# An MLP block on one core: x of three pairs transposed by DMA in place of TensorE, and two groups of sums moved forward

## The chip, the cores and the metric

The kernel runs on one core of one Trainium2 chip. The metric is the device time of one execution in microseconds (us), lower is better; each figure is a median over several executions.

## The reference

x is (8, 1024, 1024), taken as 8192 rows of 1024; w1 is 1024 x 4096, w2 is 4096 x 1024, all float32.

```python
h = x @ w1
h = 0.5 * h * (1 + np.tanh(np.sqrt(2 / np.pi) * (h + 0.044715 * h ** 3)))
return (h @ w2).astype(np.float32)
```

## The kernel before

**The two phases.** Phase one computes g = gelu(x @ w1) in 16-bit floats and stores it to DRAM (`gd`); phase two multiplies g by w2. The 8192 rows are 64 chunks `c` of 128, and two chunks make a pair `k` (32 pairs). Each row of x and each quarter of w1 is scaled by its largest absolute value before it is cast to 16 bits: a "look" finds the maximum (`look_x` on ACT; `look_w1` on DVE or ACT), a "cast" scales and converts, and the factors `us`, `rs` undo it behind the matmul. The look of a w1 quarter ends in `widest_w1` (DVE writes a tile `spread`) and `scale_w1` (one matmul on PE turns it, tile `rows`, L157); every cast of that quarter waits for it.

**Order of phase one.** w1 is split into four column quarters `r`. The first six pairs (`FIRST = 6`) run over r = 0 first, then over r = 1 and so on, while the later quarters of w1 are still being loaded; then the middle pairs run with all four quarters each, and the last four again by quarter. One (pair, quarter) is a unit `u`, 128 in all. Units 0 to 6 are `Plain`: four quarters of a product, each eight matmuls of 128x512 into PSUM banks `pa`, `pc`, `pa`, `pc` (three buffers of each), a gelu on ACT (tile `e`), a scaling cast on POOL (tile `g2`), and a store of g by SP. From unit 7 on a unit is `Quad1`: the 2x2 block product in seven products instead of eight, which needs sums of x's quarters (`sum_x`, four DVE instructions a pair, tile `xs`) and of w1's (`sum_w1`).

**x.** x arrives row by row, and TensorE needs it with the contraction on the partitions, so each cast chunk (`x16`) must be transposed into `xT`. There are two ways in the kernel. `turn_x_pe` (L204) lets TensorE transpose eight 128x128 pieces by a matmul with the identity into PSUM (tile `turned`, L211), and ACT (L216) or DVE (L218) copies that to SBUF; it serves pairs 0 to 5. `turn_x` (L198) is one DMA transpose issued by SP (L202); it serves pairs 6 to 31.

**Phase two.** 26 products for each pair (`PRODUCTS`), each of eight matmuls of 128x256. Their left factors are g's blocks, read back by DMA transposes (L511), and 18 sums of these blocks (`LEFT_SUMS`, made by `sum_g` on DVE, tiles `gs`). A row (at, node, a, b, sign) of `LEFT_SUMS` is issued just before product `at`; a negative `at` means a product of the pair before. Finished products are added into the output tiles `o` by `take`, on DVE (L532), or on ACT (L536) for the first of a block. The first products of pair 0 are interleaved with the last two units of phase one.

**What sets the order.** All five engines' queues run in the order in which the program issues (`manual_schedule`); nothing is reordered. Work beside the main stream is put into slots by `plan(u, slot, f, ...)`, and `background(u, slot)` issues what was planned. For the first units `early(p, ...)` is `plan(p // 4, p % 4, ...)`: slot `p` comes just after quarter `p` of the `Plain` units, counted from 0. Pairs 2 to 5 have their looks, casts and turns there:

```python
p = (3, 7, 11, 14)[k - 2] + h
early(p - 1, look_x, c)
early(p, scale_x, c)
early(p, cast_x, c, V)
...
early(4 * k - 2 + 2 * h, turn_x_pe, c, V if h or k == 1 else S)
```

So chunk 6 (pair 3) is looked at in slot 6, cast in slot 7 and turned in slot 10, and its first reader is quarter 12 (unit 3). In the same slots the eight loads of w1's quarter r = 1 go out on POOL's DMA queue (L261; slots 3 to 11), and their looks stand in slots 7 to 15, `widest_w1` in 16, `scale_w1` in 18. The stores of g are held back by `held` and `let_go` so that SP is not stopped by a g that is not there yet.

**Buffers.** The pool `k2` has 11 buffers of 2 KB a partition which the tiles `junk` (of the looks), `x16`, `e`, `g2` and `gs` take in turn: a new tile waits until the last reader of the tile 11 places before it is done, be that an engine or a DMA. `k4` (15 buffers) holds `xT`, `xs`, later x chunks and more.

Of the kernel before, what the change touches and what calls it, by code (L numbers as in the profile page):

```python
# [60 lines left out]
PRODUCTS = (  # L61
    (8, 35, 2, 'pa', True, ((3, 1),)), (13, 34, 1, 'pc', True, ((4, 1),)),
    (18, 23, 5, 'pb', True, ((4, 1), (5, -1))), (21, 24, 2, None, True, ((7, 1),)),
    (6, 39, 1, None, True, ((5, -1),)), (22, 12, 4, 'pa', True, ((1, -1),)),
    (25, 21, 2, None, True, ((5, -1),)), (10, 16, 6, 'pc', True, ((1, -1), (2, 1))),
    (14, 37, 1, None, True, ((1, -1),)), (24, 25, 2, None, True, ((1, -1),)),
    (2, 32, 4, None, True, ((2, 1),)), (12, 31, 3, 'pb', False, ((1, 1),)),
    (3, 17, 6, None, False, ((3, 1),)), (9, 26, 2, None, True, ((0, 1),)),
    (11, 38, 1, None, True, ((3, 1),)), (1, 47, 4, None, False, ((0, 1),)),
# [9 lines left out]
def kernel(  # L79
# [7 lines left out]
    nc = tc.nc  # L87
# [11 lines left out]
    NP = T // (2 * P)  # L99
    NR = I // 2 // N  # L100
    JR = N // P
    FIRST = 6
# [41 lines left out]
    V, S, G = nc.vector, nc.scalar, nc.gpsimd  # L144
# [372 lines left out]
    def sum_g(k, node, a, b, sign):  # L517
        t = k2.tile([P, 8, P], F16, name="gs", tag="k2")
        left[k, node] = t
        (add if sign > 0 else sub)(t, left[k, a], left[k, b])  # L520
# [27 lines left out]
    def sums_g(k, s):  # L548

        for at, *what in LEFT_SUMS:  # L550
            kk = k - at // len(PRODUCTS)
            if at % len(PRODUCTS) == s and 0 <= kk < NP and k >= 0:
                sum_g(kk, *what)

    done = [0]

    def second(n):
        for _ in range(n):
            k, s = divmod(done[0], len(PRODUCTS))
            done[0] += 1  # L560
            if s == 0 and k + 1 < NP:
                load_g(k + 1)
            sums_g(k, s)
            a, b, chain, tag, _, takes = PRODUCTS[s]
            if tag:
                chains[chain] = bank(tag)
            ps = chains[chain][:, :Q]
            x, w = left[k, a], w2set[b]
            product(ps, lambda i: x[:, i, :], [w[:, i, :] for i in range(8)], tag is not None)
            for block, sign in takes:  # L570
                take(k, block, sign, ps)
# [7 lines left out]
    at = {}  # L579
# [5 lines left out]
    def plan(u, slot, f, *args):  # L585
        assert 0 <= u, (f, args)
        todo.setdefault((u, slot), []).append((f, args))
# [6 lines left out]
    def early(p, f, *args):  # L594
        plan(p // 4, p % 4, f, *args)

    for k in range(1, FIRST):
        for h in range(2):
            c = 2 * k + h
            if k > 1:  # L600
                p = (3, 7, 11, 14)[k - 2] + h
                early(p - 1, look_x, c)
                early(p, scale_x, c)
                early(p, cast_x, c, V)
                if h:
                    early(p, factors, k, k + 1, 0)
            if k > 3:
                early((2, 5)[k - 4], load_x, c, wpool, "w")
            early(4 * k - 2 + 2 * h, turn_x_pe, c, V if h or k == 1 else S)
    for k in first:  # L610
        for i in range(4):
            if k == 1:
                early(16 + i // 2, sum_x, k, (i,))
            else:
                plan(FIRST + (k - 1) % FIRST, 2 + i, sum_x, k, (i,))

    for n in range(8):
        early((3, 4, 6, 7, 8, 9, 10, 11)[n], load_w1, 1, n)
# [30 lines left out]
    for k in list(middle) + list(last):  # L649
        a = at[k] if k in middle else at[last[0]]  # L650
        for h in range(2):
            c = 2 * k + h
# [169 lines left out]
```

## Time and profile before

| | us |
| --- | --- |
| median of three runs | 1545.39 (1545.29 to 1546.32) |
| the profiled execution | 1545.54 |
| its span | 1543.8 |
| TensorE (PE) busy in it | 1521.1 |

The first 20 us go into loading and scaling the first x and w1; phase one runs to about 817 us, phase two to the end. The granted TensorE clock is 1.00 throughout. Times in the views count from the span's start. A row of a timeline has start, duration, engine, line, operation, tile written and tiles read, and in brackets the idle time before it and what ended that. A row of the list of waits has the engine and line that waited, what it waited for, and then total, number and longest in us. PE is matmul, PEld the loading of its weights, DVE VectorE, ACT ScalarE, POOL GpSimd, SP the engine that issues most DMAs; matmuls overlap, so the distance between two starts says more than one duration.

### The profile page before, as it was taken

The numbers are of one execution on the slowest core, as the hardware profiler recorded it, in microseconds if no ns is written. First come the engines' busy times: TensorE is split into PE (matmuls) and PEld (weight loads), VectorE is DVE, ScalarE is ACT, GpSimd is POOL, SyncE is SP. The second block draws the span as 40 slices with busy tenths as digits, with TensorE's granted clock in tenths as the row PEclk, the third lists the DMA queues.
The fourth block names the chain that finished last, engine by engine and source line by source line (L and its number), as shares of the span: only waits on it lengthen the run. The fifth ranks groups of instructions, "written<-read, shape, count | busy, mean of one in ns | idle before, by whom it ended". The sixth has DMA issues, their size and how long they took to land.

```text
span 1543.8 us, 28585 instructions
## 1 busy us (share of the span) xinstructions
PE 1521.1 (99%) x10415; PEld 1015.8 (66%) x10415; DVE 1171.7 (76%) x2384; ACT 731.5 (47%) x1295; POOL 461.9 (30%) x568
## 2 busy tenths in 40 slices
PE   6999999999999999999999999999999999999999
PEld 4444444444444444444448888888888888888888
DVE  6787677777767776665238888888888888888886
ACT  6678777777777777797662111111111111111111
POOL 2767554466656665554442000000000000000000
PEclk9999999999999999999999999999999999999999
DMA  8654899878788887883799577668767766866872
GB/s 325 228 172 148 244 290 306 235 237 237 232 245 250 248 259 215 249 217 104 219 261 238 131 128 163 126 133 155 140 135 137 153 129 129 159 137 124 156 141 79
DMA packets 459804, 293.91 MB, mean 190 GB/s; under 512 B 333840, under 2 KB 427024, under 8 KB 459664
## 3 DMA queue, kind: packets, MB, share of 16 engines
q1 hardware_dynamic: 456208, 279.52, 71.4%
q0 software_dynamic: 3456, 12.58, 2.5%
q8 instruction: 81, 1.33, 0.4%
q14 instruction: 59, 0.48, 0.1%
HBM read 96.99 MB, written 114.29 MB: 137 GB/s over the span
## 4 chain that ended last, share of the span: by engine, by line
PE 94%; DMA 2%; DVE 2%; ACT 1%; issue 1%; POOL 0%; SPq 0%; ACTq 0%; POOLq 0%; DVEq 0%
PE pa L367 50%; PE pc L367 30%; PE pb L367 14%; DMA gd<-g 1%; DMA wn<-in_w_dram 1%; DVE e L163 0%; ACT w L170 0%; DVE w L166 0%; DMA xn<-in_x_dram 0%; DVE w1c L147 0%; POOL g L172 0%; DVE xs L166 0%; ACT e L414 0%; POOL wn L261 0%; PE turned L211 0%
## 5 line engine op out<-in xcount | busy, mean ns | idle before, releaser
L172 POOL TENSOR_SCALAR g<-e,rs 128x512 f16<-128x512 f32 x512 | 411.1, 814 | 355.6 <-ACT e L414 278.9
L367 PEld LDWEIGHTS <-gs 128*128 128x128 f16 x4608 | 450.7, 98 | 55.1 <-DVE gs L166 2.1
L367 PEld LDWEIGHTS <-xs 128*128 128x128 f16 x1936 | 189.3, 98 | 232.1 <-issue 2.8
L163 DVE TENSOR_TENSOR e<-pc,e 128x512 f32<-128x512 f32 x242 | 161.5, 686 | 213.4 <-ACT e L482 212.1
L367 PEld LDWEIGHTS <-xT 128*128 128x128 f16 x1676 | 163.5, 98 | 197.1 <-ACT xT L216 1.6
L367 PE MATMUL pa<-w,gs 128*128 128x256 f16 x2304 | 288.3, 273 | 1.1 <-DVE gs L166 1.1
L367 PE MATMUL pa<-w,xT 128*128 128x512 f16 x1080 | 255.7, 379 | 1.9 <-ACT xT L216 1.1
L414 ACT ACTIVATE e<-e,us 128x512 f32<-128x512 f32 x363 | 249.1, 719 | 7.7 <-DVE e L163 7.6
L367 PE MATMUL pa<-w,xs 128*128 128x512 f16 x968 | 248.4, 379 | 3.0 <-DVE xs L166 1.7
L367 PE MATMUL pc<-w,xs 128*128 128x512 f16 x968 | 248.4, 379 | 0.2 <-DVE e L163 0.2
L367 PEld LDWEIGHTS <-gT 128*128 128x128 f16 x2048 | 200.4, 98 | 23.2
L536 ACT ACTIVATE o<-pa,vo 128x256 f32<-128x256 f32 x96 | 45.2, 471 | 335.7 <-PE pa L367 333.2
L367 PE MATMUL pc<-w,gs 128*128 128x256 f16 x1536 | 194.0, 273 | 0.0
L367 PE MATMUL pa<-w,gT 128*128 128x256 f16 x1024 | 132.7, 273 | 0.0
L367 PE MATMUL pb<-w,xT 128*128 128x512 f16 x484 | 124.2, 379 | 0.0
L532 DVE SCALAR_TENSOR_TENSOR o<-pc,vo,o 128x256 f32<-128x256 f32 x160 | 77.1, 482 | 57.9 <-PE pc L367 57.9
L473 ACT COPY e<-pa 128x512 f32<-128x512 f32 x121 | 70.9, 586 | 89.8 <-PE pa L367 86.5
L166 DVE TENSOR_TENSOR gs<-gT,gs 128x1024 f16<-128x1024 f16 x160 | 109.4, 684 | 0.8 <-POOL g L172 0.5
L532 DVE SCALAR_TENSOR_TENSOR o<-pa,vo,o 128x256 f32<-128x256 f32 x192 | 92.1, 480 | 20.0 <-PE pa L367 19.7
L367 PE MATMUL pb<-w,gs 128*128 128x256 f16 x768 | 99.5, 273 | 0.4 <-DMA gd<-g 0.4
L367 PE MATMUL pc<-w,gT 128*128 128x256 f16 x768 | 99.5, 273 | 0.0
L463 ACT COPY e<-pa 128x512 f32<-128x512 f32 x121 | 69.9, 578 | 50.1 <-PE pa L367 50.1
(87 smaller groups left out, 1369.0 us busy)
## 6 DMA issues: line engine op xcount, KB each, us to landing
gd<-g SPq DMA_DIRECT2D x484, 128.0 KB, 2.9
wn<-in_w_dram SPq DMA_DIRECT2D x72, 512.0 KB, 5.5
xn<-in_x_dram SPq DMA_DIRECT2D x64, 512.0 KB, 5.3
out_dram<-o SPq DMA_DIRECT2D x62, 512.0 KB, 3.5
w<-wd SPq DMA_DIRECT2D x25, 512.0 KB, 6.2
wn<-in_w_dram POOLq DMA_DIRECT2D x24, 512.0 KB, 5.5
wd<-wt SPq DMA_DIRECT2D x24, 512.0 KB, 4.5
gd<-g SPq DMA_DIRECT2D x14, 256.0 KB, 4.7
```

The costliest lines, as they stand in the source:

```text
L163: V.tensor_tensor(out=o, in0=a, in1=b, op=ALU.add)
L166: V.tensor_tensor(out=o, in0=a, in1=b, op=ALU.subtract)
L172: G.tensor_scalar(out=o, in0=i, scalar1=s, scalar2=1.0, op0=ALU.mult, op1=ALU.mult)
L367: nc.tensor.matmul(bank, lhsT=left(i), rhs=right[i], start=start and i == 0, stop=i == n - 1, skip_group_check=True,)
L414: S.activation(out=e, in_=src, func=ACT.Gelu_apprx_tanh, scale=self.u[half])
L463: S.copy(self.e11, self.pa)
L473: S.copy(self.e12, self.pa)
L532: V.scalar_tensor_tensor(out=o, in0=ps, scalar=v, in1=o, op0=ALU.mult, op1=ALU.add)
L536: S.activation(out=o, in_=ps, func=ACT.Copy, scale=v)
```

## The change

Three edits. The x chunks of pairs 3 to 5 (6 to 11) are transposed by `turn_x` on SP instead of `turn_x_pe`, in the slot of their cast; looks and casts of pair 3 move one slot ahead, of pair 4 and 5 two (slots 6, 7; 9, 10; 12, 13). The four `sum_x` of pair 0 move from unit 11 (slots 2 to 5) to units 8 and 9 (slots 0 and 1 of each). The left sums of phase two's pair 0 with `at` of 0 or more are issued one product sooner (`AHEAD = 1`), those of later pairs as before.

```diff
         for at, *what in LEFT_SUMS:
             kk = k - at // len(PRODUCTS)
-            if at % len(PRODUCTS) == s and 0 <= kk < NP and k >= 0:
+            if at % len(PRODUCTS) == s and 0 < kk < NP:
                 sum_g(kk, *what)
-
+            if not k and at >= 0 and max(at - AHEAD, 0) == s:
+                sum_g(k, *what)
+
+    AHEAD = 1
...
             if k > 1:
-                p = (3, 7, 11, 14)[k - 2] + h
+                p = (3, 6, 9, 12)[k - 2] + h
                 early(p - 1, look_x, c)
                 early(p, scale_x, c)
                 early(p, cast_x, c, V)
...
-            early(4 * k - 2 + 2 * h, turn_x_pe, c, V if h or k == 1 else S)
+            if k < 3:
+                early(4 * k - 2 + 2 * h, turn_x_pe, c, V if h or k == 1 else S)
+            else:
+                early(p, turn_x, c, nc.sync)
     for k in first:
         for i in range(4):
             if k == 1:
                 early(16 + i // 2, sum_x, k, (i,))
+            elif k:
+                plan(FIRST + k - 1, 2 + i, sum_x, k, (i,))
             else:
-                plan(FIRST + (k - 1) % FIRST, 2 + i, sum_x, k, (i,))
+                plan(FIRST + 2 + i // 2, i % 2, sum_x, k, (i,))
```

## The prediction

> **What bounds the kernel.** The page first: who is busy, and the chain that ended last.
>
> ```profile
> PE 1521.1 (99%) x10415; PEld 1015.8 (66%) x10415; DVE 1171.7 (76%) x2384; ACT 731.5 (47%) x1295; POOL 461.9 (30%) x568
> ...
> PE 94%; DMA 2%; DVE 2%; ACT 1%; issue 1%; POOL 0%; SPq 0%; ACTq 0%; POOLq 0%; DVEq 0%
> ```
>
> TensorE is the bound: an edit pays only if it takes instructions from PE or ends one of PE's few stalls. These are in the list of waits, PE alone (total, times, longest):
>
> ```profile
> PE pa L367 <- DVE xs L166: 1.7, 1, 1.7
> PE pa L367 <- ACT e L463: 1.3, 3, 0.6
> PE pa L367 <- DVE gs L166: 1.1, 1, 1.1
> PE pa L367 <- ACT xT L216: 1.1, 1, 1.1
> PE rows L157 <- DVE spread L152: 0.8, 1, 0.8
> PE pa L367 <- ACT e L482: 0.7, 1, 0.7
> ```
>
> Three of them belong to the three edits: `xT L216` (a turned chunk copied late), `xs L166` (pair 0's x sums), `gs L166` (a left sum of phase two). PE's timeline gives the places, and the price of one turn:
>
> ```profile
> 39.72 1.89 PE L367 MATMUL pa<-w,xT 128*128 128x512 f16 x8
> 41.45 0.61 PE L211 MATMUL turned<-identity,x 128*128 128x128 f16 x8
> 41.90 1.89 PE L367 MATMUL pc<-w,xT 128*128 128x512 f16 x8
> ...
> 49.70 1.89 PE L367 MATMUL pc<-w,xT 128*128 128x512 f16 x8
> 52.70 1.90 PE L367 MATMUL pa<-w,xT 128*128 128x512 f16 x8 [1.11 <-ACT xT L216]
> ```
>
> A quarter of eight matmuls takes 1.73 us from start to start; a turn between two quarters moves the next by 41.90 − 41.45 = 0.45 (56 ns for each 128x128 piece). From 49.70 to 52.70 is 3.00, so that stall costs 1.27.
>
> Then the table by stage, for how full the DMA engines are where the new transposes go (the columns end in clock, DMA share, GB/s), and line L202, the DMA transposes that this trace has from 153.9 us on:
>
> ```profile
> 30.00:40.00 10.00, 10.00 (x65) 5.15 (x63) 5.16 (x14) 6.22 (x12) 6.93 (x10) 1.00 0.95 324
> 40.00:50.00 10.00, 10.00 (x66) 5.29 (x65) 7.47 (x15) 8.13 (x14) 6.62 (x9) 1.00 0.94 307
> 50.00:60.00 10.00, 8.89 (x55) 4.37 (x54) 7.43 (x21) 7.97 (x15) 5.15 (x6) 1.00 0.24 84
> ```
> ```profile
> L202 SPq DMA_TRANSPOSE xT<-x x52: 1237/1242/5282, 153.9 to 704.4; - x52
> ...
> DMA to landing us min/median/max: 3.0/4.9/9.2
> ```
>
> The transposes enter twenty microseconds in which the DMA engines are full; behind them lie ten that are three quarters empty.
>
> **Edit 1, what PE loses.** Six turns (48 transposing matmuls; after the quarters at 39.72, 43.62, 47.52, 52.70, 56.61, 60.63): 6 × 0.45 = −2.70. The stall before 52.70 came from a chain that ends in ACT's copy of chunk 8; that copy no longer exists: −1.27. ACT loses three copies of 1.0 us and DVE three of 0.69, work that lay beside PE: no further gain.
>
> The Trainium skill ("VectorE: DVE Perf Modes", Rules for kernel authors) speaks against this edit: turn 128x128 on TensorE when PSUM will do, at 390 ns for one piece against 1309 by DMA. Here a piece costs PE 56 ns, not 390; by the page's figure the six turns would give back about 18.7 us (an estimate), seven times what the timeline allows.
>
> **Edit 1, what it costs.** Each transpose waits only for its cast (DVE), in slots three, four or five quarters ahead of its first use. With ACT's looks and DVE's casts moved to the new slots, chunk 6 is cast by about 35.3 and issued by 36.5 (1.24 on SP's queue); the quarter that needs it is due at 43.62 − 0.45 = 43.2. So its cover is 8 us from cast to landing, where L202's rows are 3.0 to 9.2 with a median of 4.9. For chunks 7 to 11 the same count gives 9 to 12 us. I take nothing for lateness of x itself; at the 9.2 end chunk 6 would cost about 1.
>
> What the transposes displace is the larger matter. Between 1000 and 1200 us, 74,466 packets under 512 B and 17 output transfers kept the engines at 0.727; an output is as large as a load of w1, and nine of those took 38.9% of the engines in 28 to 60 us, 1.4 us each. So a small packet takes (145 − 17 × 1.4) × 16 / 74,466 = 26 ns, and a transpose of 256 KB in 256 B packets takes 1024 × 26 / 16 = 1.7 us of all 16 engines. Five transposes (chunks 6 to 10) are issued before 50 us: 8 us of work in a full stretch. Beside them run the eight loads of w1's second quarter on POOL's queue; the last lands at 50.5 in the trace. If the two queues share the displaced time evenly, it lands 4 us later, 54.5. The row matmul (58.78 before) is due at 58.78 − 1.27 − 5 × 0.45 = 55.3 and needs the last look (ACT, 1.27 with its readout) and the spread first: landing by 53.3. So PE would wait 54.5 − 53.3 = +1.2 there; the ends are 0 (the loads go first) and +5.2 (they bear all 8).
>
> The stores of g also stand behind the transposes on SP's queue, and their landing frees the k2 buffers that ACT's gelu writes; before, one such landing (6.83 us) held gelu 0.89. PSUM's six banks cover that within the block. Later POOL is the tight engine (9.92 of 10 us busy in 60 to 70) and holds the loads of w1's third quarter; PE arriving sooner does not make POOL sooner, and the 0.6 wait for `e L463` at 77.40 can grow by as much as the block gained. I take +0.5; ends 0 and +2.8.
>
> No load of x stands behind a transpose on SP's queue: chunks 10 and 11 are asked for in slots 2 and 5, ahead of the first.
>
> **Edit 2.** Pair 0's four sums move from unit 11 to units 8 and 9, well before their reader in unit 12. The stall of 1.7 at 108.34 was DVE's lateness there (DVE is busy 10.00 of 10 us from 100 to 120). What is late next is an `e` add, which PE waited 0.2 for at 113.03: −1.7 + 0 to 0.4. In the new places DVE had gaps of 1.50 and 2.77 us against 2.1 us of sums. But in unit 8 the spread before a row matmul ended only 0.23 before PE wanted it (84.07 and 84.30): two sums of 0.33 to 0.4 ahead of it cost up to 0.5; I take +0.3.
>
> **Edit 3.** Sums 24 and 25 of the first pair go one product ahead, before DVE's first `o` on bank pb instead of after it:
>
> ```profile
> 813.18 0.48 DVE L532 SCALAR_TENSOR_TENSOR o<-pb,vo,o 128x256 f32<-128x256 f32 x1
> 814.67 1.29 DVE L163 TENSOR_TENSOR e<-pc,e 128x512 f32<-128x512 f32 x2 [1.01 <-ACT e L482]
> 815.87 1.78 DVE L166 TENSOR_TENSOR gs<-gs 128x1024 f16<-128x1024 f16 x2
> ```
>
> ACT's own `o` at 813.69 waits for that `o`, and its copy of `e` at 814.06, which PE waits 0.7 for, stands behind it. Two sums ahead put both later by 1.3 to 1.7, about what the wait for `gs` (1.1) gives back: the wait changes its name. Bounds −0.7 and +0.8; I take +0.2.
>
> **The sum**, against the profiled execution's own 1545.54 (span 1543.8 and 1.7 around it; 0.15 over the median of 1545.39): −2.70 − 1.27 + 1.2 + 0.5 − 1.7 + 0.3 + 0.2 = −3.5, so 1542.1. About 0.2% (3.1 us) is what a measurement can tell from no change.
>
> **Rivals.**
> A. All hidden: w1's loads keep their landings and POOL keeps up. Then −2.70 − 1.27 − 1.7 + 0.1 = −5.6: 1540. For it: the empty stretch after 50; against: 0.95 and 0.94 before it.
>
> B. Handed back: the loads bear most of the 8 us, the row matmul stays where it was, and what edit 1 won before it is lost there. Left are the turn at 62.35 and edit 2: −0.45 − 1.4 = −1.9, with ±1.5: 1543.6.
>
> C. Slower: the queues alternate packet by packet. A 256 B packet then waits for a 4096 B packet of w1 each time. The nine loads of 128 packets above took 173 ns a packet; a transpose has 64 packets for each engine, 64 × (173 + 26) = 12.7 us. Loads left in the ring shorten that to about 10.5, past chunk 6's cover of 8 from one transpose on. The gelu of the quarter at 39.72 waits for the buffer that the transpose reads, and with it POOL, which has still two loads to issue: looks, casts and transposes of chunks 8 and 9 slip in turn. Stalls of 4 at chunk 6, 3 at chunks 7 to 9 and 2.5 at the row matmul, less the 2.7 + 1.27 + 1.4 won, make +4: 1549.5. It decides from a landing over 8 us. For it: between 34 and 37 us, with both queues full, I count 226 packets of 4096 B against 242 of 1024 B, one to one. Against: no transpose met such loads in this trace, and x transposes at full share landed by 9.2.
> The Trainium skill ("DMA: Bandwidth & Descriptors", Queues, rings and completion order) says that each engine takes turns between rows, draining a whole packet of some 9 to 17 descriptors before it switches. By that rule, if a small-element packet held that many 256 B pieces, a transpose would lose few turns, and C would shrink towards A; no run here shows which.
>
> D. Edit 3 adds its full 1.7 without return: 1543.8 for the sum, inside the range.
>
> **Chances.** Forecast (1541 to 1543.2) 0.40; A 0.15; B with D 0.25; C 0.20. The first reaches the 0.2% line (1542.3) with some two thirds: faster 0.15 + 0.28 = 0.43; same 0.12 + 0.25 = 0.37; slower 0.20. The range, 1539.6 to 1548.8, leaves out half of C and the edge of A; the likeliest case alone is 1541.0 to 1543.2.
>
> **What would show it.** Right: in PE's timeline no turned rows after 38 us and quarters 1.73 apart through 43 to 58; the row matmul at 55 to 57; the last w1 landing at 52 to 55; `xs L166` gone from PE's waits; `gs L166` gone and `e L482` near 2. Wrong: a PE wait for DMA on `xT` (C), a row matmul at 58 or later (B), L202's first landings over 8 us, or `xs` waits elsewhere.

## The result: slower, 1550.14 us

| | us |
| --- | --- |
| before, nine runs beside it | 1545.48 (1544.83 to 1546.32) |
| changed, nine runs | 1550.14 (1546.45 to 1552.39) |
| ratio | 1.0029, 95% interval 1.0019 to 1.0039 |
| profiled execution of the changed kernel | 1548.8, span 1546.9 |

The changed kernel is 4.66 us slower and its times spread over 6 us where those nine of before spread over 1.5 (in the five later groups, of 17 to 35 runs, the kernel before spread over 2 to 6). The forecast was 1542.1 with a range to 1548.8. The profiled execution is one of the quicker ones, so what it shows is less than the median's loss.

The page of the changed kernel, busy time and the chain that ended last:

```profile
PE 1521.8 (98%) x10367; PEld 1013.0 (65%) x10367; DVE 1175.9 (76%) x2381; ACT 729.1 (47%) x1292; POOL 463.0 (30%) x568
...
PE 94%; DMA 2%; DVE 1%; ACT 1%; issue 1%; POOL 0%; SPq 0%; ACTq 0%; DVEq 0%; POOLq 0%
```

PE lost 48 instructions and is still busy 0.7 us longer: some of its matmuls ran slower. In the chain, 94% is PE's own work as before. The list of waits of PE:

```profile
PE pa L367 <- DMA xT<-x: 2.4, 1, 2.4
PE pa L367 <- ACT e L463: 2.4, 4, 1.1
PE rows L157 <- DVE spread L152: 2.3, 2, 1.2
PE pa L367 <- ACT e L482: 2.0, 1, 2.0
PE pa L367 <- DVE xT L218: 0.4, 1, 0.4
PE pb L367 <- DVE gs L166: 0.3, 1, 0.3
```

The three waits that the edits aimed at (`xT L216`, `xs L166`, and `gs L166` on bank pa) are gone. In their place stand a wait for a DMA transpose, longer waits for `spread` at two row matmuls, 1.1 more for `e L463`, and a wait of 2.0 for ACT's `e` (L482) where 0.7 had been. PE's timeline of the first block:

```profile
53.00 1.89 PE L367 MATMUL pc<-w,xT 128*128 128x512 f16 x8
57.26 1.90 PE L367 MATMUL pa<-w,xT 128*128 128x512 f16 x8 [2.38 <-DMA xT<-x]
60.28 0.30 PE L157 MATMUL rows<-identity,spread 128*128 128x128 f32 x1 [1.12 <-DVE spread L152]
```

From 53.00 to 57.26 is 4.26, and a quarter takes 1.73, so PE stood 2.53 us for chunk 9, which it wanted at 54.73. The row matmul, due at 55.3 by the forecast, ran at 60.28. The table by stage and line L202 in this stretch:

```profile
40.00:50.00 10.00, 9.63 (x46) 4.18 (x45) 8.55 (x19) 6.02 (x12) 6.54 (x9) 1.00 1.17 316
50.00:60.00 10.00, 6.79 (x31) 2.73 (x29) 3.02 (x8) 5.55 (x10) 2.05 (x3) 1.00 1.10 232
```
```profile
L202 SPq DMA_TRANSPOSE xT<-x x6: 1233/1308/6349, 35.8 to 56.4; - x6
...
DMA to landing us min/median/max: 3.2/7.5/12.2
```

The ten microseconds that were three quarters empty are now full (1.10), and yet move less (232 GB/s) than the full ones of before (307). Issuing one transpose held SP's queue for up to 6.3 us, and the g stores queued behind it. The critical chain, from 38 us on, names the culprit:

```profile
38.45 6.56 DMA xT<-x
...
45.03 12.19 DMA xT<-x
...
57.26 1.92 PE pa L367 x8
```

Chunk 9 was cast by 44.12; its transpose was issued at 45.03, behind chunk 8's and a g store on SP's queue, and took 12.19 us to land. From cast to landing that is 13.1 us, where PE left 10.6.

Matched matmul by matmul, the changed kernel's PE stands against the profile of before at: +0.67 at the first row matmul (the warm-up matmuls follow each other at 0.21 us until 18.4 and at 0.11 after, where before that changed at 15.2; no edit acts yet, and of the later kernels some show 0.2 to 0.65 there and others nothing, so it is the run), +1.50 at the row matmul near 60, +1.07 after the last removed turn, +2.40 at the row matmul of unit 8, +1.43 at 114, +1.17 at 810, +2.90 from 820 on.

### The profile page after: what moved, and what is told of

Its sections match the earlier page's. It is cut to its first block, busy times and chain, and to the rows that moved or that the text cites. A ratio compares the mean times of both kernels' runs of the same rounds, so it can differ in the third digit from the quotient of the medians.

```text
span 1546.9 us, 28501 instructions
## 1 busy us (share of the span) xinstructions
PE 1521.8 (98%) x10367; PEld 1013.0 (65%) x10367; DVE 1175.9 (76%) x2381; ACT 729.1 (47%) x1292; POOL 463.0 (30%) x568
## 4 chain that ended last, share of the span: by engine, by line
PE 94%; DMA 2%; DVE 1%; ACT 1%; issue 1%; POOL 0%; SPq 0%; ACTq 0%; DVEq 0%; POOLq 0%
PE pa L367 50%; PE pc L367 30%; PE pb L367 14%; DMA xT<-x 1%; DMA wn<-in_w_dram 1%; PE pb L379 0%; DMA gd<-g 0%; DVE w L166 0%; ACT w L170 0%; DVE e L163 0%; DVE xs L166 0%; ACT e L414 0%; DVE w1c L147 0%; POOL g L172 0%; PE turned L211 0%
## 5 line engine op out<-in xcount | busy, mean ns | idle before, releaser
L166 DVE TENSOR_TENSOR gs<-gT,gs 128x1024 f16<-128x1024 f16 x160 | 109.4, 683 | 0.9 <-POOL g L172 0.5
L463 ACT COPY e<-pa 128x512 f32<-128x512 f32 x121 | 69.9, 577 | 51.7 <-PE pa L367 50.7
```

Of the source, the lines that this page charges most:

```text
L166: V.tensor_tensor(out=o, in0=a, in1=b, op=ALU.subtract)
L463: S.copy(self.e11, self.pa)
```

## The experiments

Each kernel is compared with the kernel before on the same chip, whose median was 1545.6 to 1545.9 in the five groups.

**One edit at a time.**

> Edit 1 alone (x of pairs 3 to 5 by DMA, new slots for looks and casts). Theory 1, the transposes and w1's loads hold each other up: the transpose of chunk 9 and the last load of w1's second quarter land 8 us or more after issue, PE stalls at chunk 9's first quarter and at the row matmul near 60 us, and the kernel is slower by 0 to 3 us (1545.5 to 1548.5), with the wide spread from run to run that the changed kernel has. Rival, the loss comes from edits 2 and 3: edit 1 alone is faster by 1 to 3.5 us, 1542 to 1544.5.

> Edit 2 alone (pair 0's x sums in units 8 and 9). Theory: the wait of 1.7 us for xs near 108 us goes, and up to 0.5 us comes up at the row matmul of unit 8: 1543.7 to 1544.5. Rival: the sums ahead of the spread cost the 1.2 us that the changed kernel shows at that row matmul, and the e copy is late at 108 us: 1545 to 1546.

> Edit 3 alone (left sums of phase two's first pair one product sooner). Theory: PE waits near 2 us for ACT's copy of e at the first product behind the last unit's, the granted clock falls to about half for 3 to 4 us behind this wait, and the wait for gs goes: slower by 1.5 to 2 us, 1547 to 1547.5. Rival: the lower clock belongs to other stalls of the changed kernel; then the two waits cancel, 1545.5 within 0.5.

| kernel | median | against before |
| --- | --- | --- |
| edit 1 alone | 1549.68 (1546.96 to 1552.0) | +3.95, ratio 1.0025 (1.0016 to 1.0035) |
| edit 2 alone | 1544.88 (1543.74 to 1546.79) | −0.85, ratio 0.9997 (0.9988 to 1.0006) |
| edit 3 alone | 1547.38 (1546.69 to 1550.69) | +1.65, ratio 1.0010 (1.0001 to 1.0019) |

They add up to +4.75, as much as the loss. Edit 1 came out 1.2 past what theory 1 gave it. Its profile shows why, in PE's waits and in the table by stage (the third column from the end is the granted clock):

```profile
PE pa L367 <- DMA xT<-x: 3.5, 1, 3.5
```
```profile
55.00:58.00 3.00, 0.00 (x0) 0.00 (x0) 0.67 (x2) 0.00 (x0) 0.00 (x0) 1.00 1.10 134
58.00:61.00 3.00, 2.66 (x8) 0.81 (x8) 0.43 (x3) 2.79 (x6) 1.36 (x2) 0.69 1.19 312
61.00:64.00 3.00, 2.83 (x11) 1.32 (x12) 2.90 (x11) 2.48 (x5) 2.76 (x4) 0.74 0.40 134
```

PE stands for 3.5 us, and then runs at a granted clock of 0.69 and 0.74 in the next six. The stall costs more than itself: the two quarters behind it took 2.66 and 2.46 us where 1.89 is usual, 1.3 together.

Edit 2 wins less than the 1.4 of the forecast, and the interval includes no gain at all: PE's waits for `e L463` grew from 1.3 (three) to 2.4 (four) in sum, the largest, 1.1, where the wait for `xs` had been. That is the second half of the rival. Its first half is out: PE passes the row matmul of unit 8 0.09 sooner than before.

Edit 3's profile has these two waits:

```profile
PE pa L367 <- ACT e L482: 2.0, 1, 2.0
...
PE pa L367 <- ACT o L536: 0.9, 1, 0.9
```

The 2.0 is as forecast; the wait for `gs` on bank pa is gone, and 0.9 for ACT's `o` stands in its place. The clock did not fall in this execution, the quickest of edit 3's runs; in the changed kernel's, it did. The changed kernel's timelines of DVE, ACT and PE, and its table by stage:

```profile
814.29 1.49 DVE L166 TENSOR_TENSOR gs<-gs 128x1024 f16<-128x1024 f16 x2
815.69 0.48 DVE L532 SCALAR_TENSOR_TENSOR o<-pb,vo,o 128x256 f32<-128x256 f32 x1
```
```profile
816.20 0.47 ACT L536 ACTIVATE o<-pb,vn 128x256 f32<-128x256 f32 x1 [4.15 <-DVE o L532]
816.58 0.58 ACT L482 COPY e<-pa 128x512 f32<-128x512 f32 x1
```
```profile
817.20 1.84 PE L367 MATMUL pa<-w,xT 128*128 128x512 f16 x4 [2.03 <-ACT e L482]
```
```profile
815.00:818.00 3.00, 0.97 (x5) 0.26 (x4) 1.90 (x4) 1.80 (x4) 0.17 (x1) 0.88 1.25 211
818.00:821.00 3.00, 3.00 (x15) 1.86 (x14) 2.46 (x5) 2.14 (x5) 3.00 (x4) 0.55 0.98 185
```

Two sums, `o`, ACT's `o`, ACT's `e`, PE: the chain is the one in the forecast. Behind it the four matmuls took 1.84 instead of 1.03.

**Which two sums.** The condition keeps sums 24 and 25 at their product: `max(at - AHEAD * (what[0] not in (24, 25)), 0) == s`.

> Edit 3 alone, but sums 24 and 25 stay at product 3, behind DVE's o on bank pb; the other sums of the first pair are one product sooner. Theory: these two carry edit 3's whole loss, so PE's wait for ACT's e falls back to 0.7 and the wait for gs stays near 1: 1545.2 to 1546. Rival: the other moved sums make DVE's o late as well: 1546.5 or more.

1545.59 (1544.24 to 1549.72), ratio 1.0000: the theory holds, moving these two is what loses in edit 3, and the rest of edit 3 does nothing that the times show.

**The other way round.** `at += not k and (at, what[0]) in ((2, 9), (2, 22))` ahead of the condition of before.

> The opposite of edit 3: in the kernel before, sums 9 and 22 of phase two's first pair are made one product later (3 instead of 2), behind DVE's o on bank pb. Theory of edit 3 (DVE's o, then ACT's o, then ACT's copy of e form a chain to PE, and every sum ahead of it is paid by PE): the wait for e L482 (0.7 to 0.85 at 814.7) goes, the wait for gs gets shorter: 1543.8 to 1544.8. Rival: sums 22, 24 and 25 are late and the gs wait grows by as much: 1545.5 or more.

1545.86 (1544.98 to 1549.52), ratio 1.0002. The wait for `e L482` is gone from the list, as the theory says, but the time did not follow: `gs` on bank pa still costs 1.1, and a wait for another left sum, on bank pb, is 1.5 in this profile, with DVE waiting 1.78 for a buffer that POOL frees. Over the kernels of this case that wait on bank pb was 0 to 2.9 in the profiles, so a gain under 1 us is not to be seen here.

**Part of edit 1.** Only pair 5 (`if k < 5` keeps the turn), or only pair 3 (`if k != 3`, with its slots of edit 1):

> Only pair 5 (chunks 10 and 11) by DMA, in the old slots of look and cast (14 and 15); pairs 3 and 4 stay on TensorE. These two transposes are issued after about 52 us, when w1's loads are nearly all in. Theory 1: no contention, both land within 4 us, two turns of 0.45 us go and nothing comes back: 1544.3 to 1544.9. Rival, a DMA transpose hurts whatever runs beside it: 1545.5 or more.

> Only pair 3 (chunks 6 and 7) by DMA, in edit 1's slots; pairs 4 and 5 stay on TensorE in their old slots. Theory 1: two transposes land in 6 to 8 us, in time for PE; w1's last loads land about 2 us later than before, still in time or nearly, so two turns (0.9) go and up to 0.9 comes back: 1544.8 to 1545.8. Rival, two transposes among the loads are enough for the harm: 1546.5 or more.

Pair 5: 1545.46 (1544.53 to 1549.73), ratio 1.0002 (0.9993 to 1.0010). Its two transposes landed in 3.16 and 3.07 us, so they met no contention; 0.65 of the 0.9 of turns shows in the median span (1543.3 against 1543.95), but 0.5 of it comes back outside the span (2.26 around it against 1.77), which I cannot explain.

Pair 3: 1553.01 (1551.23 to 1555.46), ratio 1.0047: worse than all six transposes, and the rival's side. ACT's waits between 40 and 60 us, and the table by stage:

```profile
ACT junk L270 <- DMA gd<-g: 4.4, 1, 4.4
...
ACT junk L185 <- DMA gd<-g: 1.2, 1, 1.2
```
```profile
40.00:45.00 5.00, 4.81 (x23) 2.22 (x24) 3.46 (x6) 3.42 (x6) 3.55 (x6) 1.00 1.23 115
```

With the DMA engines busy throughout, they moved 115 GB/s. In these 5 us one transpose's 1024 packets took 70 ns each and w1's 4096 B packets 348, where 26 and 173 had gone into the forecast. The g stores behind them landed after up to 13.1 us and ACT stood for the buffers they hold. Chunk 8's turn ends in a copy on ACT, behind these waits; PE stood 7.0 for it, and ran at a clock of 0.50 after. With all six by DMA there is no such copy, which may be why that version loses less: no run separates it.

**Contention by itself.** The new slots, PE's turns kept, and each chunk also sent into its pair's `xs` tile, by `dma_start_transpose`, or by two plain `dma_start`:

> The kernel before with edit 1's new slots; each of chunks 6 to 11 is transposed by DMA as in edit 1, but into the pair's xs tile, which nobody reads until the sums overwrite it, and TensorE still turns x as before. So PE keeps its six turns (2.7 us) and waits for no DMA transpose; what the transposes do to w1's loads, to g's stores and to the buffers stays. Theory 1, contention: the last w1 load lands at 55 us or later, the row matmul waits 1 us or more, 1547 to 1550. Rival, only the late landing of chunk 9 itself costs (PE waits for xT): the row matmul is on time and the time is 1545 to 1546.

> As the experiment with both, but each DMA transpose is replaced by two plain copies of the same chunk into the same tile (1.4 to 1.7 us of all 16 engines at the rate of other transfers, as much engine time as one transpose). If engine time alone matters, w1's loads land as late as with transposes: 1547 to 1550. If it is the transposing that slows what runs beside it, w1's packets keep 160 to 220 ns, the last load lands by 54 us, and the time is 1545 to 1546.5.

Transposes as well: 1559.98 (1554.07 to 1560.55), ratio 1.0085. The direction is theory 1's, the price 10 beyond it: PE waited 10.0 for ACT's copy of chunk 8. Plain copies: 1554.85 (1553.66 to 1555.83). Neither expectation fits, and the run does not separate them: the second copy into the same tile waits on SP for the first to land, so the g stores were late again, and PE waited 7.3 for the same copy. What it does show is that w1 hardly suffered beside copies that wait for each other: its last load landed at 52.7 (51.6 before, 58.95 with transposes).

**One queue.** What POOL issues goes over the queue that the profile calls software_dynamic, what SP issues over hardware_dynamic, and the profile counts both against the core's 16 DMA engines. `(G if r > 1 else nc.sync).dma_start(...)` in `load_w1` puts w1's second quarter on SP's hardware queue, in program order with transposes and stores. First edit 1 alone, then its control without edit 1, then pair 3 alone:

> Edit 1 alone with one thing changed: the eight loads of w1's second quarter are issued by SP, on the same hardware queue as the transposes and g's stores, instead of by POOL on the software queue. Theory 1a, the loss comes from w1's packets and the transposes' packets taking turns on the same DMA engines from two queues (the stretches of 115 to 160 GB/s): in one queue they do not mix, no stretch from 36 to 56 us falls under 250 GB/s, no landing is over 9 us, PE waits for no chunk, and the time is 1542.5 to 1545. Theory 1b, it is the amount of work alone: landings of 10 us or more and PE's stall near 55 us stay, 1547 to 1551.

> Control for the experiment with one queue: the kernel before with w1's second quarter loaded by SP, nothing else changed. Theory 1a and 1b alike: no transposes there, so little changes, 1544.5 to 1546.5; if SP, waiting to issue a load, holds up g's stores, 1547 or more.

> Pair 3 alone by DMA, as before, but w1's second quarter is loaded by SP, so that loads and transposes share one queue. Theory 1a (two queues that mix): the transposes land within 6 us, no g store takes over 9, PE's stall of 7 us at chunk 8 is gone, 1543.5 to 1545.5. Rival (order of the buffers and of ACT's work with these slots): the stall stays and the time is over 1548.

| kernel, w1 by SP | median | same with w1 by POOL |
| --- | --- | --- |
| edit 1 alone | 1544.85 (1543.37 to 1548.95) | 1549.68 |
| without edit 1 | 1544.92 (1544.47 to 1545.57) | 1545.78 |
| pair 3 alone | 1544.45 (1543.97 to 1545.31) | 1553.01 |

The table by stage for pair 3 in one queue, the same stretch as above:

```profile
40.00:45.00 5.00, 4.80 (x23) 2.20 (x24) 3.43 (x6) 3.47 (x6) 1.74 (x3) 1.00 1.10 304
```

115 GB/s became 304, the two transposes landed in 3.2 and 4.2 us, and ACT waits for no store. So in these kernels the harm came only with two queues: transposes on the hardware queue while w1 comes over the software queue. Two limits on that: on SP's queue w1's packets are 2048 B, not 4096, and the loads are issued in SP's order, which this test changes too, so that the number of queues is not shown apart from these; and in the profile of edit 1 in one queue small packets still took 57 ns each between 45 and 50 us and one 5 us stretch moved 233 GB/s, so the part of expectation 1a that no stretch falls under 250 failed. No transpose there took over 7.7 to land.

**Where edit 1's gain goes in one queue.** Edit 1 in one queue gained nothing on its control (1544.84 and 1544.92), though PE has 2.7 us less to do. Its profile's waits show what takes it:

```profile
PE rows L157 <- DVE spread L152: 2.5, 3, 1.5
```

The last w1 load landed at 55.8 and the row matmul waited 1.5. So the loads were issued sooner: slots `(2, 3, 4, 5, 6, 7, 8, 9)` for `(3, 4, 6, 7, 8, 9, 10, 11)`, with edit 2 in all of these:

> Edit 2 with w1's second quarter loaded by SP, no x by DMA in these pairs: the measure for the next two. If the parts add up: 1544.9 − 0.85 = 1544.1.

> Edits 1 and 2, w1's second quarter loaded by SP. If the row matmul takes back what the turns gave: within 0.5 of edit 2 with w1 by SP, 1543.6 to 1544.5. If one queue lets edit 1 pay: 1542.5 or less.

> As edits 1 and 2 in one queue, but the loads of w1's second quarter are issued in slots 2 to 9 instead of 3 to 11. If the late last load is what takes edit 1's gain: it lands by 54, the wait for spread at the row matmul near 57 us falls from 1.5 to under 0.5, and the time is 1 to 1.5 us below the run with edits 1 and 2, 1542.5 to 1543.3. Rival: transposes, now behind more loads, land late and PE waits for xT: 1544.5 or more.

> The control for the run with sooner loads: edit 2 and w1's second quarter by SP in slots 2 to 9, x of pairs 3 to 5 turned by TensorE in the old slots. If edit 1 is what pays there (2.7 us of turns, 0.5 to 1.3 of the stall at chunk 8), this is slower by 1.5 to 2.5: 1543.4 to 1544.4. Rival, the sooner loads do it alone: within 0.5 of 1542.0.

| edit 2, w1 by SP | old load slots | sooner |
| --- | --- | --- |
| without edit 1 | 1543.63 (1543.19 to 1544.55) | 1543.62 (1543.26 to 1544.6) |
| with edit 1 | 1544.05 (1543.19 to 1546.72) | 1541.99 (1541.14 to 1544.74) |

With sooner loads the last one landed by 50.8, PE had no wait for a DMA transpose, and the row matmul ran at 55.70 without a wait, 3.1 sooner than before. Sooner loads alone do nothing; edit 1 alone does nothing; together they give 1.6 (1.4 when each is taken against the kernel before on its own chip). The time is 0.5 under what was expected. This version (edits 1 and 2, one queue, sooner loads) beats both kernels: ratio 0.9978 (0.9969 to 0.9987) to the kernel before. What is left of the rows waits, 1.1 in sum, is 0.9 at unit 8 and 0.2 at the first row matmul:

```profile
PE rows L157 <- DVE spread L152: 1.1, 2, 0.9
```

**Combinations.** Edit 2, pair 5 by DMA and sums 9 and 22 later; and the best version with these sums later:

> Edit 2, pair 5 alone by DMA in the old slots, and sums 9 and 22 one product later, together. If the parts add up: 1545.6 − 0.85 (edit 2) − 0.3 to 1.0 (pair 5) − 0.8 to 1.8 (sums) = 1542 to 1543.7, faster than both kernels.

> The run with edits 1 and 2, one queue and sooner loads, and sums 9 and 22 one product later. If the wait for e L482 (0.4 to 0.85) is removed without return: 1541.2 to 1541.7; if the gs wait behind it grows: 1542.0 or more.

The first gave 1545.17 (1543.42 to 1547.39), ratio 0.9993: the parts did not add up, and no single one of them is above what the runs can tell. The second gave 1541.98 (1540.59 to 1544.32), the same as without the sums.

## Why the prediction was wrong, point by point

**What edit 1 takes from PE: right.** The turns are gone and quarters follow each other at 1.73 from 42.64 to 53.00; the stall at chunk 8 is gone. At 53.00 the changed kernel stood 1.88 ahead of before although it had started 0.67 and a 0.37 wait for chunk 5's copy behind.

**"I take nothing for lateness of x itself": the step that failed first.** The cover of chunk 9 was about right (10.6 us of the 9 to 12 given); the landing was 12.2 after the issue, outside L202's rows of before (3.0 to 9.2), which had been measured beside hardware transfers only, and PE stood 2.53 us. The text of rival C said that no transpose there met software loads, and the sum went by those rows all the same. Edit 1 alone in two queues cost +3.95 where the sum had −2.3 (−2.70 − 1.27 + 1.2 + 0.5).

**w1's loads, +1.2: mis-sized, and its start was off.** The last one landed at 56.7; I had 54.5, from a landing before of 50.5 that the trace gives as 51.6. The displaced time was 5.0, between the even share (4) and all of it (8). With the 2.0 that the forecast took from landing to row matmul, this landing by itself would have put the row matmul at 58.7, an estimate. It ran at 60.28, 5 us after its due time, of which 2.5 is chunk 9 and 0.67 the start. What ended its wait in this profile was not w1's landing but ACT's last look, which stood behind a gelu:

```profile
57.32 0.69 ACT L402 ACTIVATE e<-pa,us 128x512 f32<-128x512 f32 x1 [1.05 <-DMA xT<-x]
58.48 1.06 ACT L270 ACTIVATE junk<-wn 128x1024 bf16<-128x1024 f32 x1
```

By the profile, that gelu was released by the landing of chunk 9's transpose, which had been reading the buffer (in edit 1's own profile ACT stood 5.8 us at this place). So chunk 9 was paid by PE directly, and again by way of ACT. And it did not end there: the loads of w1's third quarter were issued at 61.9 instead of 58.8, DVE waited 9.7 us in all for w1's loads, and the row matmul of unit 8 lost another 1.3 where +0.5 and +0.3 stood in the sum. Alone, edit 1 and edit 2 show almost no wait there (0 and 0.03 in their profiles, 0.3 for edit 1 in one queue), the two together in one queue do (2.0); which of the late loads and edit 2's sums costs it is not separated.

**Rival C: right in its side, wrong in how the packets mix.** Its wait of gelus for the buffer that a transpose reads did come (3.1 us in sum between 40 and 60 us), but packets did not alternate one to one. From 37.5 to 43 us transposes and loads ran in turns (from 39.0 on: 0.6 us of transposes, 1.5 of loads, 0.5 of transposes), at 35 and 181 ns a packet, and chunks 6 and 7 landed in 7.0 and 6.6, in time. From 49.5 to 56 they ran side by side and both slowed, w1's 4096 B packets to 326 ns, one of them to 2.4 us. In the one-queue runs the late landings are gone, within the limits said there; why packets of the two slow each other is not shown. The page of the Trainium skill that I set against C ("DMA: Bandwidth & Descriptors", Queues, rings and completion order) has each engine drain a packet and then switch rows; the turns could fit that, though no row shows where such a packet ends, and the stretch with packets of 326 ns is nothing that it speaks of.

**Edit 2, −1.4: its median is −0.85, 0.55 less of a gain, and not clear of no change.** The wait for `xs` went as said. What is late next was not the 0.2 at 113 but ACT's `e` at the same place, 1.1.

**Edit 3, +0.2: mis-sized at +1.65.** The bound given was +0.8. The chain and its 1.3 to 1.7 were right (the wait for `e L482` rose by 1.3); "about what the wait for gs gives back" was not: at product 6, where the wait for `gs` of 1.1 is gone, PE waits 0.9 for ACT's `o` in edit 3's profile and pays the clock in the changed kernel's.

**Two slips that move nothing in the sum.** The 1152 packets of the software queue between 28 and 60 us are eight loads, 1024 packets of 4096 B at 193 ns and 128 of 4 B, not nine loads at 173 ns; with that an output is 1.56 us instead of 1.4, a small packet 25.5 ns instead of 26, and C's transpose 14.0 us instead of 12.7. And D counts edit 3's 0.2 twice: it gives 1543.6.

**Not in the sum at all: the clock.** In the changed kernel all nine runs have a mean granted clock under 1.000, with an average of 0.998; of the 32 runs of before beside the first group, six have. Half speed for t us lowers the mean by 0.5 t / 1548, so 0.002 is some 6 us at half speed and 3 us lost, an estimate from rounded means. That is nearly what lies between the profiled execution and the slowest runs (3.6), but it does not order the runs: the two slowest, 1552.39 and 1552.3, have 0.998 and 0.999, and the two with 0.997 took 1551.24 and 1551.4. So what else makes the spread is not shown. Whether a stall of 2 us is followed by a slow stretch differed between executions: 2.03 was in the changed kernel's profile, 2.02 was not in edit 3's.

## What to carry to other kernels

A landing time read from one traffic mix is no bound for another: before a transfer is moved into a full stretch, ask which queue its neighbours use. Here, with eight loads on a software queue, putting them in the same hardware queue as the transposes, in the order in which they are needed, took the harm away. When an instruction leaves the bound engine, the next thing due there must come sooner too, or the gain waits at it: here the removed turns paid only once w1's loads were moved up. And work put ahead of an in-order engine's short link to the bound engine (two sums ahead of `o`) cost nearly its full length here: 1.3 us more wait for two sums of 1.49 together.

## What was not expected of the hardware

The granted TensorE clock fell after short waits: 0.88 and 0.55 in the six microseconds around a wait of 2.03, 0.69 and 0.74 after one of 3.5, 0.50 after one of 7.0; but it stayed 1.00 after a wait of 2.38 in the same profile as the first, and after one of 2.02 in edit 3's. The Trainium skill ("TensorE: Matmul & The Clock Gate", Why this matters for your kernels) asks for no idle gaps over about 3 us; here the clock fell after a wait of 2.0 in one execution.

Busy DMA engines do not mean moved bytes: 1.23 of share with 115 GB/s, and 1.10 with 304, in the same stretch of two kernels that differ in the queue of eight loads, and so in their packets' size.
